# A second bias buffer and a norm in line in the last block, and scaled rows that stand behind VectorE's last instruction that is no tap

## The chip, the core and the metric

The kernel runs on one core of one Trainium2 chip. The time is device microseconds (us) of one execution; the median of several runs is compared. One core has five engines that matter here, each with a queue of its own and semaphores between them: TensorE (PE in the profile; PEld are its weight loads), VectorE (DVE), ScalarE (ACT), GpSimd (POOL) and SyncE (SP), which here only issues DMA transfers. Data are in DRAM, in the on-chip memory SBUF, and in PSUM, the banks that TensorE writes to.

## The reference, cut to what matters

One layer of a streaming encoder, for 2048 prompt frames and 64 sample frames, in float32 with D = 1024:

```python
h = rms_norm(x, norm1_g) * (1 + sc1) + sh1
glu_a, glu_b, q, k, v, g_conv, g_attn = split(h @ w_in)
u = glu_a * sigmoid(glu_b)                    # 512 channels
y = causal_depthwise_conv(u, width=31) + b_dw
y = silu(layer_norm(y, ln_g, ln_b))           # "the convolution's norm"
conv_out = y @ w_conv_out
q, k = rms_norm(q, per head), rms_norm(k, per head)   # 8 heads of 64
s = q @ k.T / 8 + rel_bias[clipped distance]; masked to 9 chunks of 64
attn_out = (softmax(s) @ v) @ w_attn_out
merged = sigmoid(g_conv) * conv_out + sigmoid(g_attn) * attn_out
x = x + gt1 * (merged @ w_o)
x = x + gt2 * swiglu_ffn(rms_norm(x) * (1 + sc2) + sh2)
```

The bias depends on the head and on the distance alone, so a tile of 128 queries against 640 keys needs one 128x640 tile of bias per head.

## The kernel before, in words

**Arithmetic.** Each float32 operand is split into a high and a low part (ScalarE copies the high part, rounded; VectorE or GpSimd subtracts it from the value), and a product is three products of parts. `split` and `low` do this; names end in `hi`/`lo`, `part_h`/`part_l`, `ph`/`pl`.

**Stages.** The first phase goes through the frames in four blocks b = 0 to 3 (`PBLOCKS`; the first holds the 64 sample frames and 512 prompt frames, the others 512). Each block has the stages q, 0, k, 1, v, 2, 3, g: the projections to q, k and v, between them the four channel tiles of the convolution's input (0 to 3), and at the end 16 gate tiles (g). The second phase (three blocks, `CBLOCKS`) reads the results back from DRAM: the norm's output from `c_d`, the attention's from `o_d`, the gates from `g_d`, and does merge, output projection and FFN. Phase one ends and phase two begins at about 1164 us of the span.

**What runs beside the projections.** Python generators, in lanes (`Lane`): the norm of the next block's rows, the scaling and storing of q, k, v rows (`work`), the attention's heads (`attn`, two at a time), the convolution (`conv`), and the convolution's norm (`tail`). After each TensorE instruction given, the planner (`Stream`) pumps the lanes: a generator goes on when the value it yielded is due. `stream.load[engine]` is the planner's own estimate of when the engine will be through with what it was given; `stream.when("act", "dve")` is the latest of several engines' estimates, and as a due time it is compared with TensorE's. `stream.at(t, f)` runs `f`, mostly a store, once TensorE's estimate has passed `t`.

**The order on the engines.** TensorE's instructions run in the order in which the program gives them (`manual_schedule` for PE). The order on VectorE, ScalarE, GpSimd and SyncE is chosen by the language's scheduler; `tc.issue_after(ins)` adds an edge: what is given under it stands behind `ins` in the order. `Meter` is the wrapper of each engine through which all compute instructions are given (its call is line 105, so nearly all rows of the profile say L105); it notes the instruction given last as `.last`.

**Scaled rows.** `qk_rows` handles a tile of 128 rows of q or k: ScalarE squares, VectorE sums per head (`ssq`, then `t`), GpSimd takes the root with a power (`r<-t,mhalf`), VectorE multiplies the rows by it (`kn<-kn,r`), TensorE transposes them (`store_kq`: `pt<-ident,kn`), ScalarE and VectorE split the result (`part_h`, `part_l`), SyncE stores it. The multiplication is given under `tc.issue_after(dve.last.ins)`: behind the instruction that VectorE was given last, whatever that is.

**The convolution.** `convolve` gives 31 instructions per channel tile on VectorE (`y<-u,wd,y`, a *tap* each; 0.8 us for 512 to 606 columns). They are the filling of VectorE: a tap is given whenever the planner has VectorE less than 2 us loaded, up to four in a row.

**The convolution's norm.** `conv_norm` waits until the block's taps are given, sums over the channels on GpSimd and TensorE (means, then squares), takes the root, and then goes through the four channel tiles one after the other: GpSimd multiplies (`y<-y,s`, all four given at the start), ScalarE's tanh (`ln<-y,lnh`), two steps of VectorE, the two parts (`part_h`, `part_l`), and stores to `c_d`. Between the steps it yields, so a tile takes four turns of the planner.

**Attention.** `attend` does one head: it waits until the head before has given all its scores; then `fetch` loads the bias (`load_bias`, two DMAs into the one tile `bias`, so they can't start before the last reader of the former bias is through) and q and k, and the scores wait for a due time `BIAS_LAG` = 6 us of the planner behind that load. For each of four tiles of 128 queries: scores (`sc`) on TensorE, sum with the bias and maximum in one VectorE instruction (`pr<-sc,bias`), exponential on ScalarE (`pr<-pr,sm`), transposes (`ptp`), parts, and the product with v (`po`). Two heads together give one 128x512 tile of output (`o_p`), split and stored to `o_d`. Blocks 0 to 3 have eight heads each, block 0 the sample's eight as well; a block's heads run beside the next block's stages, and block 3's beside its own gates.

**The last gate stage.** From the v stage of block 3 on, `attn` gives up to two steps per turn. In the gate stage `spare["open"]` is true for b >= 2 (the last block: until gate tile 6), which lets a head load the next head's q and k early. At gate tile 10 of block 3 the program gives all heads for which q and k were loaded early, closes the pool `wa` and takes its memory for the first loads of the merge. After the last gate the remaining head, taps and norm are drained, and the merge starts.

Of the kernel before, what the change touches and what calls it, by code (L numbers as in the profile page):

```python
# [8 lines left out]
F32 = mybir.dt.float32  # L9
# [613 lines left out]
def streaming_layer(ctx: ExitStack, tc: tile.TileContext, I, O):  # L623
# [392 lines left out]

    bias = wk.tile([P, 640], F32, name="bias")
    begun_rows = []
# [255 lines left out]
    def convolve(u, y, ct, b):  # L1274
# [13 lines left out]
        dve.tensor_scalar(y[:, ct, :n], u[:, :n], wd[:, ct, 0:1], bdw[:, ct : ct + 1], ALU.mult, ALU.add)  # L1288
        for k in range(1, TAPS):
            with tc.issue_after(ahead_of_taps[-1]) if ahead_of_taps else nullcontext():  # L1290
                dve.scalar_tensor_tensor(
                    y[:, ct, :n], u[:, k : k + n], wd[:, ct, k : k + 1], y[:, ct, :n], ALU.mult, ALU.add
                )
            yield

    def conv_norm(y, c0, n, t0):
        yv = y[:, :, c0 : c0 + n]
# [32 lines left out]
        yield stream.when("dve")  # L1330
        done = []
        for ct in range(4):
            gps.tensor_tensor(yv[:, ct], yv[:, ct], s[:, :n], ALU.mult)
            done.append(stream.when("pool"))
        for ct in range(4):
            yield done[ct]
            tmp = temp("ln")
            act.activation(tmp[:, :n], yv[:, ct], AF.Tanh, bias=lnh[:, 4 + ct : 5 + ct], scale=lnh[:, ct : ct + 1])
            yield stream.when("act")
            dve.tensor_scalar(yv[:, ct], yv[:, ct], lng[:, ct : ct + 1], lnb[:, ct : ct + 1], ALU.mult, ALU.add)  # L1340
            dve.scalar_tensor_tensor(tmp[:, :n], tmp[:, :n], 1.0, yv[:, ct], ALU.add, ALU.mult)
            yield stream.when("dve")
            hi, lo = parts()
            act.activation(hi[:, :n], tmp[:, :n], AF.Copy)
            yield stream.when("act")
            name = low(hi[:, :n], lo[:, :n], tmp[:, :n], n, TT_LESS)

            def store(ct=ct, hi=hi, lo=lo):
                for l, a in enumerate((hi, lo)):
                    nc.sync.dma_start(c_d[l, ct, :, t0 : t0 + n], a[:, :n].bitcast(F32))  # L1350

            stream.at(stream.when(name), store)

    def gates(b, free):
# [109 lines left out]
    def spans(b):  # L1464
# [4 lines left out]
        return SMP + QB * b, QB, CACHE + SMP + QB * b - past, QB + past  # L1469

    def load_bias(h):
        for r in (0, HD):
            nc.sync.dma_start(
                bias[r : r + HD, HD - r : 640 - r],
                bass.AP(tensor=rb_d.tensor, offset=rb_d.offset + 768 * h + HD, ap=[[1, HD], [1, 576]]),
            )
        return bias
# [33 lines left out]
    def attend(i):  # L1511
# [136 lines left out]
    for b, stage in ORDER:  # L1648
# [21 lines left out]
        elif stage == "g":  # L1670
            spare["open"] = b >= 2
            for g in gates(b, free):
# [20 lines left out]
        else:  # L1693
# [7 lines left out]
            if stage == 3:  # L1701
# [680 lines left out]
```

## Time and profile before

| | |
|---|---|
| median of 3 runs | 2945.38 us (2942.96 to 2947.97) |
| the profiled execution's own time | 2941.67 us |
| span of its profile | 2939.5 us |
| TensorE busy | 2889.3 us, 98% |
| VectorE busy | 2053.9 us, 70% |
| ScalarE busy | 1362.7 us, 46% |
| GpSimd busy | 1164.9 us, 40% |
| mean granted TensorE clock | 0.997 |

How to read it: the span runs from the first to the last instruction of the program in one profiled execution; the execution's own time is 2.2 us longer. The busy share is a mean over stages with different limits: TensorE has something to do nearly everywhere, so what matters is where it stands idle, and for what. A row of the waits names the instruction that came late to TensorE and the engine that it came from. A row of the timeline is: start in us, duration, engine, line, operation, output and inputs by the program's names, shape, and in square brackets the idle time just ahead and what ended it. The granted clock is the share of full speed that the chip granted TensorE in a stretch.

### The profile page before, as it was taken

What the parts mean: (1) busy time and instruction counts of PE and PEld (TensorE: products, weight loads), DVE (VectorE), ACT (ScalarE), POOL (GpSimd) and SP (SyncE); (2) the same over time, 40 slices, a digit from 0 to 9 for tenths busy, and PEclk for the clock granted to TensorE, in tenths of its full rate; (3) what the DMA queues carried; (4) which work ended last, traced back from release to release, by engine and by line L of the source; (5) the groups of instructions that cost most, each with busy time, mean ns of one, the idle gap of its engine ahead of it and who ended that gap; (6) DMA issues with size and microseconds to landing.
All of it is one profiled execution on the core that took longest, in us unless ns stands there. A gap on an engine that the chain in (4) does not pass through costs nothing.

```text
span 2939.5 us, 44832 instructions
## 1 busy us (share of the span) xinstructions
PE 2889.3 (98%) x16193; PEld 2587.5 (88%) x16193; DVE 2053.9 (70%) x3648; ACT 1362.7 (46%) x2453; POOL 1164.9 (40%) x753
## 2 busy tenths in 40 slices
PE   7999999999999999999999999999999999999999
PEld 5899777888888887988999998999999999999998
DVE  5897788668967885577777756666666557566666
ACT  3346543751564266563444345444444345444442
POOL 1201210111011002553566452366567742465667
PEclk9999999999999999999999999999999999999999
DMA  9989899978996987984444875332333965333333
GB/s 322 315 305 314 287 281 329 285 232 306 285 297 197 320 270 224 291 295 157 144 144 146 292 261 200 97 122 94 115 115 104 346 220 179 97 103 106 115 107 127
DMA packets 467067, 628.04 MB, mean 214 GB/s; under 512 B 36196, under 2 KB 314584, under 8 KB 466845
## 3 DMA queue, kind: packets, MB, share of 16 engines
q1 hardware_dynamic: 452944, 606.11, 63.4%
q10 hardware_dynamic: 13901, 19.08, 1.9%
q8 instruction: 127, 2.08, 0.3%
q14 instruction: 95, 0.78, 0.1%
HBM read 476.53 MB, written 148.54 MB: 213 GB/s over the span
## 4 chain that ended last, share of the span: by engine, by line
PE 47%; DVE 2%; ACT 1%; DMA 1%; issue 1%; POOL 0%; SPq 0%; ACTq 0%; DVEq 0%; POOLq 0%
PE ps L105 29%; PE pd L105 13%; PE pw L105 5%; DVE wlo L105 1%; ACT whi L105 1%; DVE ps L105 0%; DMA cin<-o_d 0%; DMA x<-x_d 0%; DVE acc L105 0%; ACT xn L105 0%; DMA wst<-in_w_ffn_in 0%; DMA wfo<-in_w_ffn_out 0%; DMA tg<-g_d 0%; DVE sums L105 0%; PE pt L105 0%
## 5 line engine op out<-in xcount | busy, mean ns | idle before, releaser
L105 PE MATMUL ps<-t,whi 128*128 128x384 f32 (+1 forms) x2112 | 502.0, 322 | 2.8 <-ACT u L105 1.7
L105 POOL TENSOR_TENSOR wlo<-wst,whi 128x1024 fp32r<-128x1024 f32 (+1 forms) x159 | 362.7, 2293 | 246.1 <-ACT whi L105 214.4
L105 ACT ACTIVATE whi<-wst 128x1024 fp32r<-128x1024 f32 (+1 forms) x265 | 258.3, 979 | 316.1 <-PE ps L105 129.6
L105 PE MATMUL ps<-b,whi 128*128 128x384 f32 (+1 forms) x1584 | 380.7, 325 | 6.4 <-DVE v L105 2.1
L105 PEld LDWEIGHTS ps<-t,whi 128*128 128x128 f32 x2112 | 367.8, 188 | 10.1 <-ACT u L105 3.9
L105 DVE SCALAR_TENSOR_TENSOR y<-u,wd,y 128x512 f32<-128x512 f32 (+1 forms) x480 | 370.1, 774 | 8.0
L105 PE MATMUL ps<-hh,whi 128*128 128x512 f32 (+2 forms) x992 | 362.8, 366 | 0.1
L105 DVE TENSOR_TENSOR acc<-acc,pd 128x512 f32<-128x512 f32 x482 | 322.2, 685 | 48.1 <-PE pd L105 45.6
L105 PE MATMUL ps<-hh,wlo 128*128 128x512 f32 (+2 forms) x992 | 345.2, 348 | 0.0
L105 PE MATMUL ps<-hl,whi 128*128 128x512 f32 (+2 forms) x992 | 344.5, 347 | 0.0
L105 PE MATMUL ps<-t,wlo 128*128 128x384 f32 (+1 forms) x1056 | 338.5, 321 | 0.0
L105 PE MATMUL pd<-whi,hid 128*128 128x512 f32 x912 | 297.9, 391 | 0.6 <-DVE hid L105 0.3
L105 PEld LDWEIGHTS ps<-b,whi 128*128 128x128 f32 x1584 | 276.9, 188 | 14.6 <-DVE v L105 3.2
L105 ACT ACTIVATE pr<-pr,sm 128x640 f32<-128x640 f32 (+3 forms) x272 | 201.9, 749 | 137.1 <-DVE sm L105 134.8
L105 PE MATMUL ps<-b,wlo 128*128 128x384 f32 (+1 forms) x792 | 256.1, 323 | 0.0
L105 POOL TENSOR_TENSOR r<-t,mhalf 128x1 f32<-128x1 f32 (+2 forms) x68 | 82.3, 1219 | 403.7 <-DVE t L105 377.8
L105 PEld LDWEIGHTS ps<-hh,wlo 128*128 128x128 f32 x992 | 186.5, 188 | 22.6
L105 DVE TENSOR_TENSOR wlo<-wst,whi 128x1024 fp32r<-128x1024 f32 (+1 forms) x106 | 135.9, 1286 | 100.3 <-ACT whi L105 98.9
L105 PEld LDWEIGHTS pd<-whi,hid 128*128 128x128 f32 x912 | 171.2, 188 | 37.2 <-DVE acc L105 1.8
L105 PEld LDWEIGHTS ps<-hh,whi 128*128 128x128 f32 x992 | 187.0, 189 | 18.2 <-issue 3.3
L105 PEld LDWEIGHTS ps<-hl,whi 128*128 128x128 f32 x992 | 187.4, 189 | 14.3 <-issue 1.7
L105 PEld LDWEIGHTS ps<-t,wlo 128*128 128x128 f32 x1056 | 198.2, 188 | 0.8
(233 smaller groups left out, 6309.6 us busy)
## 6 DMA issues: line engine op xcount, KB each, us to landing
whi<-w_din_h SPq DMA_DIRECT2D x72, 512.0 KB, 6.4
wlo<-w_din_l SPq DMA_DIRECT2D x72, 512.0 KB, 7.3
wst<-sum_d SPq DMA_DIRECT2D x131, 256.0 KB, 3.1
wfo<-in_w_ffn_out SPq DMA_DIRECT2D x64, 512.0 KB, 4.1
wmod<-in_w_ada SPq DMA_DIRECT2D x46, 512.0 KB, 8.8
sum_d<-ws SPq DMA_DIRECT2D x88, 256.0 KB, 2.0
wst<-in_w_ffn_in SPq DMA_DIRECT2D x85, 256.0 KB, 3.2
wst<-in_w_in SPq DMA_DIRECT2D x40, 512.0 KB, 6.0
```

Of the source, the lines that this page charges most:

```text
L105: self.last = f(*args, **kw)
```

## The change

Three parts.

*Scaled rows.* In `convolve` the tap no longer counts as the instruction given last: `dve.last` is put back to what it was before each tap. So `kn<-kn,r` in `qk_rows`, and the other places that use `dve.last`, stand behind the last instruction of VectorE that is not a tap (nor the first product of a channel tile's convolution, which still counts).

*A second bias buffer.* In the last block's gate stage, up to gate tile 6, `spare["open"]` has the value "wide". As a head starts its scores there, it loads not only the next head's q and k but also its bias, into a second tile taken from pool `wa` under tag "x" (three slots that also hold v rows and some k rows). The two corners of it that the loads don't reach are filled with a large negative number, once. A head that finds its bias loaded takes the due time of that load.

*The norm's line.* In the last block, `conv_norm` no longer goes through the channel tiles one after the other. In round i = 0 to 6 it gives the parts and stores of tile i-3, the two VectorE steps of tile i-2, the tanh of tile i-1 and GpSimd's product of tile i, and yields once between rounds, until the planner's latest estimate of ScalarE, VectorE and GpSimd. In the other blocks the same steps are given in the same order as before.

```diff
@@ convolve
         for k in range(1, TAPS):
+            other = dve.last
             with tc.issue_after(ahead_of_taps[-1]) if ahead_of_taps else nullcontext():
                 dve.scalar_tensor_tensor(
                     y[:, ct, :n], u[:, k : k + n], wd[:, ct, k : k + 1], y[:, ct, :n], ALU.mult, ALU.add
                 )
+            dve.last = other
             yield
@@ conv_norm
-    def conv_norm(y, c0, n, t0):
+    def conv_norm(y, c0, n, t0, line=False):
...
+        tmps = [None] * 4
+
+        def over(ct):
+            gps.tensor_tensor(yv[:, ct], yv[:, ct], s[:, :n], ALU.mult)
+
+        def swish(ct):
+            tmps[ct] = temp("ln")
+            act.activation(tmps[ct][:, :n], yv[:, ct], AF.Tanh, bias=lnh[:, 4 + ct : 5 + ct], scale=lnh[:, ct : ct + 1])
+
+        def times(ct):
+            tmp = tmps[ct]
+            dve.tensor_scalar(yv[:, ct], yv[:, ct], lng[:, ct : ct + 1], lnb[:, ct : ct + 1], ALU.mult, ALU.add)
+            dve.scalar_tensor_tensor(tmp[:, :n], tmp[:, :n], 1.0, yv[:, ct], ALU.add, ALU.mult)
+
+        def give(ct):
+            tmp = tmps[ct]
+            hi, lo = parts()
+            act.activation(hi[:, :n], tmp[:, :n], AF.Copy)
+            if not line:
+                yield stream.when("act")
+            name = low(hi[:, :n], lo[:, :n], tmp[:, :n], n, TT_LESS)
...
+            stream.at(stream.when(name), store)
+
+        if line:
+            for i in range(7):
+                if 0 <= i - 3:
+                    yield from give(i - 3)
+                for step, ct in ((times, i - 2), (swish, i - 1), (over, i)):
+                    if 0 <= ct < 4:
+                        step(ct)
+                if i < 6:
+                    yield stream.when("act", "dve", "pool")
+            return
@@ load_bias
+    second = {}
+
     def load_bias(h):
+        bias = first_bias
+        if spare["open"] == "wide" and now["bias"] is not None and now["bias"][1] is first_bias:
+            bias = second.get("tile")
+            if bias is None:
+                bias = second["tile"] = wa.tile([P, 2, 512], F32, tag="x", name="bias", bufs=3)[:].rearrange("p a b -> p (a b)")[:, :640]
+                for r, c in ((0, 0), (HD, 576)):
+                    dve.memset(bias[r : r + HD, c : c + HD], BIG)
@@ fetch
-            if now["bias"] is None or now["bias"][0] != h:
+            told = now.pop("next", None)
+            landed = stream.load["pe"] + BIAS_LAG
+            if told is not None and told[0] == i:
+                now["bias"], landed = told[1:3], told[3]
+            elif now["bias"] is None or now["bias"][0] != h:
                 now["bias"] = h, load_bias(h)
...
-            loaded[i] = max(stream.load["pe"] + BIAS_LAG, ahead_qk.get(i, stream.load["pe"] + lag))
+            loaded[i] = max(landed, ahead_qk.get(i, stream.load["pe"] + lag))
@@ attend
             fetch_qk(i + 1)
             ahead_qk[i + 1] = stream.load["pe"] + QK_LAG
+            if spare["open"] == "wide":
+                now["next"] = i + 1, order[i + 1][1], load_bias(order[i + 1][1]), stream.load["pe"] + BIAS_LAG
@@ the stages
-            spare["open"] = b >= 2
+            spare["open"] = b >= 2 and ("wide" if b == len(PBLOCKS) - 1 else "narrow")
...
-                    tail.add(conv_norm(y, 0, QB, lo))
+                    tail.add(conv_norm(y, 0, QB, lo, b == len(PBLOCKS) - 1))
```

More of the change, by code (lines that the diff above doesn't have):

```diff
@@ L1015, in first_block @@
         next(taps, None)
-    bias = wk.tile([P, 640], F32, name="bias")
+    first_bias = bias = wk.tile([P, 640], F32, name="bias")
     begun_rows = []
@@ L1336, in conv_norm @@
             yield done[ct]
-            tmp = temp("ln")
-            act.activation(tmp[:, :n], yv[:, ct], AF.Tanh, bias=lnh[:, 4 + ct : 5 + ct], scale=lnh[:, ct : ct + 1])
+            swish(ct)
             yield stream.when("act")
-            dve.tensor_scalar(yv[:, ct], yv[:, ct], lng[:, ct : ct + 1], lnb[:, ct : ct + 1], ALU.mult, ALU.add)
-            dve.scalar_tensor_tensor(tmp[:, :n], tmp[:, :n], 1.0, yv[:, ct], ALU.add, ALU.mult)
+            times(ct)
             yield stream.when("dve")
[L1343 to L1352, printed above, removed]
+            yield from give(ct)
     def gates(b, free):
```

5 lines of the change are left out of this document (4 added, 1 removed).

## The prediction

> **What bounds the kernel now.** I read the page first, then the waits of TensorE, then the timelines of the two places where it waits longest and the change acts.
>
> ```profile
> span 2939.5 us, 44832 instructions
> PE 2889.3 (98%) x16193; PEld 2587.5 (88%) x16193; DVE 2053.9 (70%) x3648; ACT 1362.7 (46%) x2453; POOL 1164.9 (40%) x753
> ...
> PE pt L105 <- DVE kn L105: 6.1, 2, 4.0
> PE ps L105 <- DVE t L105: 5.8, 5, 3.4
> PE sc L105 <- DVE sm L105: 2.7, 5, 1.3
> ```
>
> TensorE is busy for 98% of the span: 50 us are idle in all (2939.5 - 2889.3), and its work is the same after the change. So the change can only win or lose idle time of TensorE, and the clock that goes with it. The wait rows (engine and tile, who ended the wait, us in total, times, longest) name rows kn (6.1 us in two waits) and t (longest 3.4 us).
>
> ```profile
> 1157.02 0.33 PE L105 MATMUL ptp<-ident,pr 128*128 128x128 f32 x1 [0.50 <-ACT pr L105]
> 1158.76 0.50 PE L105 MATMUL po<-pl,vv 128*128 128x512 f32 x1 [0.22 <-DVE pl L105]
> 1162.55 0.45 PE L105 MATMUL po<-pl,vv 128*128 128x384 f32 x1 [0.28 <-DVE pl L105]
> 1164.57 0.41 PE L105 MATMUL ps<-cin,whi 128*128 128x320 f32 x1 [1.40 <-DVE o_p L105]
> 1175.29 0.90 PE L105 MATMUL ps<-cin,whi 128*128 128x320 f32 x2 [3.42 <-DVE t L105]
> ```
>
> These are the five waits at the passage from the projections to the merge (start, duration, instruction, idle time before it and its releaser). The first three and the fourth are the last attention head, alone on TensorE when the gates are through (0.50 + 0.22 + 0.28 = 1.00 us, and 1.40 us for its output o_p, whose PSUM bank the merge takes over). The fifth is VectorE's first merge product. Why that was late:
>
> ```profile
> 1169.59 2.79 DVE L105 TENSOR_TENSOR part_l<-ln,part_h 128x512 fp32r<-128x512 f32 x1 [0.70 <-DMA o_d<-part_l]
> 1174.75 0.49 DVE L105 SCALAR_TENSOR_TENSOR t<-tg,ps 128x320 f32<-128x320 f32 x1 [2.38 <-DMA c_d<-part_l]
> ...
> 1172.40 0.32 SPq L1350 DMA_DIRECT2D c_d<-part_l  x1
> ...
> L105 ACT ACTIVATE ln<-y,lnh x4: 800/808/821, 1130.1 to 1163.8; 128x512 f32<-128x512 f32 x4
> ```
>
> The convolution's norm is still at its last channel tile. Its four tanhs run from 1130.1 to 1163.8, one per 11.2 us, though each is 0.81 us of work; the last lower part ends at 1172.38, its store is issued at 1172.40, and t, which takes over that memory, starts when the store has landed.
>
> ```profile
> 1170.53:1173.95 3.42, 1.34 (x10) 1.08 (x8) 1.84 (x1) 0.00 (x0) 1.29 (x1) 1.00 0.23 84
> 1173.95:1180.78 6.83, 5.49 (x20) 5.49 (x21) 3.43 (x8) 0.86 (x3) 0.00 (x0) 0.50 0.91 273
> 1180.78:1187.61 6.83, 6.83 (x48) 6.80 (x48) 2.50 (x8) 3.53 (x5) 5.79 (x3) 1.00 1.03 341
> ```
>
> Stretches of time: length, busy time and instructions of TensorE, weight loads, VectorE, ScalarE, GpSimd, then the granted clock. After 3.42 us with only 1.34 busy the clock is 0.50 for 6.83 us. There 20 matmuls took 5.49 us; the next 6.83 us hold 48 of the same, so 20 are worth 2.85 us, and the half clock cost 2.64 us.
>
> **The change part by part: the norm's line.** The steps and their instructions are the same 4 x (GpSimd multiply, tanh, two VectorE steps, two halves, two stores); only the order is new: one round does the next step of up to four tiles, and there are 6 pauses in place of 15. A pause is now as long as the planner holds the fullest of three engines loaded, for which I take 3 us, from the longest chain of a round (the 0.81 tanh and, as an estimate from t's 0.49 on 320 columns, 0.5 to 0.8 for each of its three VectorE instructions). From the multiplies at 1126.9 (below) that gives the last tile at about 1126.9 + 6 x 3 = 1145, its stores landed some 6 us later, 1151: ahead of the last gate. So t and the queue no longer wait: -3.42 us and, with the idle stretch gone, -2.64 us.
>
> ```profile
> 1126.89 4.66 POOL L105 TENSOR_TENSOR y<-y,s 128x512 f32<-128x512 f32 x4
> 1169.43 2.39 POOL L105 TENSOR_TENSOR wlo<-wst,whi 128x1024 fp32r<-128x1024 f32 x1 [5.71 <-ACT whi L105]
> c_d<-part_h SPq DMA_DIRECT2D x16, 256.0 KB, 6.1
> ```
>
> The four multiplies took 4.66 us in a row and now run beside VectorE's products. The long part_l above (2.79 us) ends 0.56 us after GpSimd's wlo of 1169.43 does (1171.82). The Trainium skill, "SBUF — State Buffer", section "Who interferes with whom", says that a VectorE instruction with two SBUF inputs and a GpSimd instruction that reads SBUF lock each other out for a whole instruction; this row agrees, and by that rule the line meets up to three such locks of about 1.2 us, 3.6 us on a chain that by the sum ends 11 us early, so the sum stays.
>
> **The second bias buffer.** A head's bias is loaded one head ahead, into a spare 128x1024 slot, in the gate stage's first part; two memsets of 64x64 on VectorE are added at the first of them (under the 0.49 us of t above each, with VectorE a quarter idle there), the number of loads stays.
>
> ```profile
> 1075.52 0.81 DVE L105 CUSTOM_DVE_ANT_0 pr<-sc,bias 128x640 f32<-128x640 f32 x1
> 1076.36 1.10 SPq L1473 DMA_DIRECT2D bias<-rb_d  x2
> 1081.58 0.81 DVE L105 CUSTOM_DVE_ANT_0 pr<-sc,bias 128x640 f32<-128x640 f32 x1
> 1122.84 0.83 DVE L105 CUSTOM_DVE_ANT_0 pr<-sc,bias 128x640 f32<-128x640 f32 x1 [0.18 <-DMA bias<-rb_d]
> ```
>
> A head's last score maximum is at 1075.52, the next bias is asked for at 1076.36, the next head starts at 1081.58, 6.06 us on. From there to 1122.84 two heads pass, 20.6 us each; less a turn of 6.06 that is 14.6 us for three steps from tile to tile, 4.9 us at most. So 1 to 2 us are won per head, and more where a head waits for the bias itself (that of 1122.84), whose planned time now counts from a load one head earlier: an estimate of 15 us over the last five, between 6 and 25. The last head, whose o_p let the merge go on at 1164.57, is through near 1150, beside the gates: -1.00 us, and of the 1.40 I keep half (the merge's first bank may then wait for ScalarE to read the last gate; bounds 0 and 1.40): -0.70 us. The loads are moved past the q, k and v loads on SyncE's queue; 1.10 us of issue per head either way, with nobody waiting there.
>
> What it adds: heads that stand closer. ScalarE's work per head is 11.1 us:
>
> ```profile
> L105 ACT ACTIVATE pr<-pr,sm 128x640 f32<-128x640 f32 x56 | 46.0, 827 | 20.3 <-DVE sm L105 19.9
> L105 ACT ACTIVATE ph<-ptp 128x512 fp32r<-128x512 f32 x38 | 22.0, 593 | 13.6 <-PE ptp L105 13.5
> L105 ACT ACTIVATION_READ_ACCUMULATOR pr<-pr,sm 128x1 f32 x28 | 5.2, 187 | 0.0
> L105 ACT ACTIVATE other<-po 64x512 f32<-64x512 f32 x7 | 4.2, 593 | 0.2
> ```
>
> (46.0 + 22.0 + 5.2 + 4.2)/7 heads. With 18 us from head to head that leaves room; with 13 and a gate's 0.6 it is 90% full. The trace does not show such a stretch. Bounds: 0, and the longest wait for a maximum (1.3 us) once in five heads, 6.5 us. I take 1.0, nearer the short end, since TensorE's row of waits has only 2.7 us of that kind for all 40 heads.
>
> **Scaled rows.** In block 0 to 3 rows of the k stage are queued behind the last tap given. The one that matters:
>
> ```profile
> 99.88 0.17 DVE L105 TENSOR_SCALAR t<-ssq 128x8 f32<-128x8 f32 x1
> 100.20 3.76 POOL L105 TENSOR_TENSOR r<-t,mhalf 128x8 f32<-128x8 f32 x2 [4.30 <-DVE t L105]
> 105.83 0.69 DVE L105 TENSOR_TENSOR part_l<-pt,part_h 128x512 fp32r<-128x512 f32 x1 [1.59 <-ACT part_h L105]
> 107.80 0.84 DVE L105 SCALAR_TENSOR_TENSOR y<-u,wd,y 128x606 f32<-128x606 f32 x1
> 108.56 0.69 DVE L105 TENSOR_TENSOR kn<-kn,r 128x512 f32<-128x512 f32 x1
> 109.40 0.41 PE L105 MATMUL pt<-ident,kn 128*128 128x128 f32 x2 [2.15 <-DVE kn L105]
> 106.44:209.05 102.61, 100.46 (x658) 92.62 (x657) 100.67 (x151) 38.13 (x66) 12.58 (x10) 1.00 0.91 312
> 212.82 0.44 PE L105 MATMUL sc<-kk,q 128*128 128x384 f32 x1 [0.26 <-DVE sm L105]
> ```
>
> This root was done at half of 3.76 us, 102.1, the row was scaled at 108.56 behind a tap, and TensorE stood 2.15 us. Freed of the tap it fits into the 1.59 us in which VectorE waited, and the 2.15 us go. But from 106.44 to 209.05 VectorE is busy for 100.67 of 102.61 us, and at 212.82 TensorE waits for it: what it won it gives back there, save the 0.69 us that moved into the idle slot. Against that, a row that is placed ahead of its root holds every tap behind it:
>
> ```profile
> 918.84 0.69 DVE L105 TENSOR_TENSOR kn<-kn,r 128x512 f32<-128x512 f32 x1 [1.81 <-POOL r L105]
> ```
>
> 1.81 us once, and block 0 has three such rows: +5.4 us less the 1.59 us idle and the 0.69, about +3. Bounds -2.15 and +3, middle near 0; I take 0. In blocks 1 to 3 no wait of TensorE hangs on such a row (the second kn wait, 3.96 us at 360.51, stands behind a store, below, not behind a tap).
>
> **Sum.** -3.42 - 2.64 - 1.00 - 0.70 + 1.0 + 0 = -6.8 us. The profiled execution took 2941.67 us (2.2 us around its span), 3.7 us less than the median of 2945.38. Against the median: 2938.6 us, -0.23%. What a measurement tells from no change is about 0.2%, 5.9 us, so faster begins at 2939.5 and slower at 2951.3.
>
> **The rivals.** First: the passage waits for something else. Weights (wlo, 2.39 us above) or the gate rows tg of the merge, loaded only two tiles ahead, may be late next. Then the 3.42 us and the clock are won in part; at half of the 6.06 us the time is 2941.6. For it: ScalarE's and VectorE's work there is unchanged; against it: SyncE's queue is freed too, as its store at 1172.40 no longer holds it.
>
> Second: the root holds VectorE in block 0, the +3 us above: 2941.6.
>
> Third, on the slower side: halves that wait for stores. The norm's halves share two buffers with the heads' outputs and the queries; the line gives them 3 us apart, so a buffer is asked for again after 6 us, and a store lands after 6.1 us at the median.
>
> ```profile
> 358.26 0.69 ACT L105 ACTIVATE part_h<-pt,gqk 128x512 fp32r<-128x512 f32 x1 [1.10 <-DMA c_d<-part_h]
> 362.54 0.69 ACT L105 ACTIVATE part_h<-pt,gqk 128x512 fp32r<-128x512 f32 x1 [3.59 <-DMA c_d<-part_h]
> 360.51 0.63 PE L105 MATMUL pt<-ident,kn 128*128 128x128 f32 x4 [3.96 <-DVE kn L105]
> ```
>
> This is block 0's norm drained in a burst: ScalarE stood 1.10 and 3.59 us for stores, VectorE behind it, TensorE 3.96 us. With 2.64 us of half clock that is 6.6 us each time; two such stops in the last block cost 13.2 us, and with the gain of 6.8 the time is 2951.8. It decides when a head is still under way as the halves come; by the sum the heads end near 1150 and the halves come from 1136, so it can be, though gates alone would not mind.
>
> That the change does little (the order on the engines falls out as before): 2944.
>
> The Trainium skill, "TensorE: Matmul & The Clock Gate", section "What's actually happening", has the clock fall after an idle window of 3.4 us that runs freely. Here it fell 2.08 us into the idle time, after a window that was 39% busy; by the page's rule a stop of 3.96 us need not cost a half clock at all, and the slower rival would come to 7.9 us, 2946.5.
>
> **How the numbers follow.** Forecast 0.42 (2934 to 2940); passage in part 0.20; root in block 0 0.10; little changed 0.08; halves that wait for stores 0.20 (two stops; three would be 2958). Faster by over 0.2%: the forecast, 0.40 (its upper end lies past the bound); within 0.2%: 0.40, that end and the three cases in between; slower 0.20. For 8 in 10 the range goes from 2932 (nothing paid for closer heads, and the 2.15 us kept in part) to 2952 (two stops). The forecast's own range is 2934 to 2940.
>
> **What would show it.** Right: no wait of TensorE above 1 us between 1150 and 1185 and a clock of 1.00 there; the last tanh of the norm before 1150; the last o_p before the last gate; the wait at 107 gone and a wait for a maximum near 183 to 213 grown. Wrong: VectorE idle for r in the k stages; part_h waiting for c_d; new waits for pr, sm or pl in the last block; TensorE waiting for m, tg or weights after 1165. An order of instructions on VectorE that changes elsewhere, in blocks 1 and 2, would be outside all of this and could cost a few us either way.

## The result

Over 20 runs each, the changed kernel takes 2948.35 us (median; 2942.93 to 2954.69) and the kernel before 2943.03 us (2939.88 to 2947.97). The ratio is 1.0017, with an interval of 1.0011 to 1.0023: about 5.0 us slower, by less than the 0.2% that the prediction took as its bound. Forecast were 2938.6 us, 6.8 us faster than before, with a range from 2932 to 2952. The time lies in the range, but on the other side of the kernel before.

The profiled execution of the changed kernel took 2944.85 us (before: 2941.67). From its page, the span and the engines, and from the waits of TensorE the three rows that answer to those shown of before:

```profile
span 2943.0 us, 44833 instructions
PE 2887.1 (98%) x16193; PEld 2585.9 (88%) x16193; DVE 2054.9 (70%) x3650; ACT 1362.3 (46%) x2453; POOL 1163.7 (40%) x753
PE pt L105 <- DVE kn L105: 8.1, 2, 6.6
PE ps L105 <- DVE t L105: 4.0, 4, 3.2
PE sc L105 <- DVE sm L105: 4.0, 4, 2.1
```

The work is the same and TensorE is idle for 55.9 us (2943.0 - 2887.1), 5.7 us more than before. The waits for rows (kn) grew from 6.1 to 8.1 us, those for maxima (sm) from 2.7 to 4.0, and the one for t that the change was expected to remove went only from 3.4 to 3.2. The waits themselves, from TensorE's timeline (start, duration, instruction, in brackets the idle time ahead of it and who ended it):

```profile
126.29 0.30 PE L105 MATMUL pt<-ident,kn 128*128 128x128 f32 x1 [1.49 <-DVE kn L105]
308.85 0.80 PE L105 MATMUL sc<-kk,q 128*128 128x256 f32 x2 [2.13 <-DVE sm L105]
367.00 0.45 PE L105 MATMUL pt<-ident,kn 128*128 128x128 f32 x1 [6.57 <-DVE kn L105]
1165.96 0.39 PE L105 MATMUL ps<-cin,whi 128*128 128x320 f32 x1 [1.08 <-DVE row L105]
1176.49 0.90 PE L105 MATMUL ps<-cin,whi 128*128 128x320 f32 x2 [3.24 <-DVE t L105]
```

Set side by side by TensorE's instructions, the changed kernel is 1.1 us behind at 50 us (waits at the kernel's start, which differ from execution to execution), 1.3 us ahead at 108 us (the wait of 2.15 us is gone), 0.35 behind at 126, 2.35 at 309, 6.5 at 367, 3.5 at 401, 4.2 at 975, 1.4 at 1166 and 2.4 at TensorE's last instruction (3.5 by the span). So the loss is made between 126 and 370 us, in block 0. The last block, for which two of the three parts were made, wins 2.8 us, of which the second phase gives 1.0 back.

At the passage to the merge, groups of ScalarE's and VectorE's instructions in the changed kernel (count, least/median/longest duration in ns, first and last start):

```profile
L105 ACT ACTIVATE ln<-y,lnh x4: 802/807/816, 1152.2 to 1162.8; 128x512 f32<-128x512 f32 x4
L105 DVE SCALAR_TENSOR_TENSOR y<-u,wd,y x63: 730/752/755, 999.7 to 1109.9; 128x512 f32<-128x512 f32 x63
L105 DVE CUSTOM_DVE_ANT_0 pr<-sc,bias x28: 760/818/827, 1033.9 to 1144.1; 128x640 f32<-128x640 f32 x28
```

the same two groups of VectorE before the change:

```profile
L105 DVE SCALAR_TENSOR_TENSOR y<-u,wd,y x60: 730/752/929, 1002.7 to 1089.2; 128x512 f32<-128x512 f32 x60
L105 DVE CUSTOM_DVE_ANT_0 pr<-sc,bias x28: 808/815/828, 1029.1 to 1153.4; 128x640 f32<-128x640 f32 x28
```

and the timeline of GpSimd and VectorE after it:

```profile
1166.43 8.00 POOL L105 TENSOR_TENSOR wlo<-wst,whi 128x1024 fp32r<-128x1024 f32 x3 [11.07 <-ACT whi L105]
1166.90 5.30 DVE L105 TENSOR_TENSOR part_l<-ln,part_h 128x512 fp32r<-128x512 f32 x2 [0.49 <-ACT part_h L105]
1175.94 0.49 DVE L105 SCALAR_TENSOR_TENSOR t<-tg,ps 128x320 f32<-128x320 f32 x1 [3.34 <-DMA c_d<-part_h]
```

The heads do end earlier: their last maximum is at 1144.1 in place of 1153.4. The four tanhs do run in a line, 10.6 us from first to last in place of 33.7. But the last tap of the convolution moved from 1089.2 to 1109.9, the norm behind it starts that much later, and its last two lower parts take 5.30 us for the two, beside three subtractions of GpSimd. The store of these parts is as late as before, t waits for it, and the clock (third column from the right, ahead of DMA share and GB/s) falls as before:

```profile
1171.97:1175.38 3.41, 1.28 (x9) 1.01 (x7) 0.64 (x2) 0.00 (x0) 2.46 (x1) 1.00 1.01 381
1175.38:1182.21 6.83, 5.72 (x21) 5.72 (x22) 3.61 (x10) 1.09 (x3) 0.00 (x0) 0.50 0.95 286
```

### The profile page after: what moved, and what is told of

It is laid out like the page before. It is cut to its first block, busy times and chain, and to the rows that moved or that the text cites. A ratio compares the mean times of both kernels' runs of the same rounds, so it can differ in the third digit from the quotient of the medians.

```text
span 2943.0 us, 44833 instructions
## 1 busy us (share of the span) xinstructions
PE 2887.1 (98%) x16193; PEld 2585.9 (88%) x16193; DVE 2054.9 (70%) x3650; ACT 1362.3 (46%) x2453; POOL 1163.7 (40%) x753
## 4 chain that ended last, share of the span: by engine, by line
PE 47%; DVE 2%; ACT 1%; DMA 1%; issue 1%; POOL 0%; SPq 0%; ACTq 0%; DVEq 0%; POOLq 0%
PE ps L105 28%; PE pd L105 13%; PE pw L105 5%; DVE wlo L105 1%; ACT whi L105 1%; DVE ps L105 0%; DMA cin<-o_d 0%; DMA x<-x_d 0%; DMA wst<-in_w_conv_out 0%; ACT xn L105 0%; DMA tg<-g_d 0%; DMA wfo<-in_w_ffn_out 0%; DVE acc L105 0%; DVE sums L105 0%; PE pt L105 0%
```

## The experiments

Times are medians, each beside runs of the kernel before on the same chip (2942.4 to 2943.3 us). Brackets hold the 95% interval of the ratio, and a difference with a sign is that ratio in us. "The page" below is that of the profile.

### The parts one by one

**Rows alone.** The change with its first part only.

```diff
+            other = dve.last
             ... the tap ...
+            dve.last = other
```

> The scaled rows alone. Theory 1 (the new order on VectorE in blocks 0 and 1 is where the time goes): slower than before by 3.5 to 5 us, as the changed kernel's profile is 3.5 us behind at 470 us of the span; the wait for kn near 360 us stands at 5 us or more. Theory 2 (the closer heads of the last block are the cost): within 1.5 us of before. My forecast for this part was 0, between -2.15 and +3.

Measured: 2949.71 us, ratio 1.0023 [1.0015, 1.0032]: +6.8 us. The first part, which the sum took at nothing, costs no less than the whole change.

**Bias buffer alone.** The second tile and the early load, neither rows nor line.

```diff
-            spare["open"] = b >= 2
+            spare["open"] = b >= 2 and ("wide" if b == len(PBLOCKS) - 1 else "narrow")
```

> The second bias buffer alone. Theory 1: within 1.5 us of before: what the last head no longer waits (2.4 us) is lost again as the taps, and so the norm, come later. Theory 2: slower by 3 us or more, with the norm's first tanh some 20 us later than at 1130 and a longer wait for t. My forecast for this part was -0.7 (-1.00 -0.70 +1.0).

Measured: 2945.2 us, 1.0008 [0.9999, 1.0017]. The interval leaves both theories open. The convolution's last tap starts at 1103.2 in place of 1089.2, the norm's first tanh at 1147.9 in place of 1130.1, and TensorE waits 3.44 us for t, as before.

**Line alone.**

```diff
-                    tail.add(conv_norm(y, 0, QB, lo))
+                    tail.add(conv_norm(y, 0, QB, lo, b == len(PBLOCKS) - 1))
```

> The norm's line alone. If the line does what I forecast: the last tanh ends before 1150, the waits for t (3.4 us) and the half clock behind it (2.64 us) go, 4 to 6 us faster. If its place depends on when the taps are through and not on its own pauses: the last tanh stays near 1160, t waits as before, within 1.5 us of before.

Measured: 2943.03 us, 1.0001 [0.9993, 1.0010]. The tanhs are through before 1150, as the prediction asked, though the last tile's lower part starts at 1152.45 and not at about 1145; and yet nothing is won. ScalarE's group:

```profile
L105 ACT ACTIVATE ln<-y,lnh x4: 802/802/836, 1132.8 to 1144.5; 128x512 f32<-128x512 f32 x4
```

the longest of TensorE's waits there:

```profile
1162.07 0.47 PE L105 MATMUL ptp<-ident,pr 128*128 128x128 f32 x1 [2.44 <-ACT pr L105]
```

and two stretches of time (columns as in those shown of before):

```profile
1158.20:1161.60 3.40, 1.18 (x7) 0.89 (x7) 1.44 (x7) 3.38 (x7) 2.35 (x1) 1.00 0.22 89
1161.60:1168.40 6.80, 6.09 (x24) 5.20 (x25) 2.77 (x4) 3.52 (x6) 0.00 (x0) 0.50 0.32 105
```

The wait of 3.42 us for t is gone, as forecast. In its place the last head is later, TensorE runs out of other work around 1160 while ScalarE is busy for 3.38 of 3.40 us, and the half clock falls there, 12 us earlier than before, with another 3.4 us of it at 1171.9.

**Bias buffer and line, no rows.** The change without the two lines of the first experiment.

> Bias buffer and line together, without the scaled rows. Theory 1: -1 to +1.5 us against before, that is the changed kernel less the 3.5 to 5 us of the rows; the norm's first tanh near 1150, part_l locked for 5 us and t waiting 3 us as in the changed kernel. Theory 2: as slow as the changed kernel, +4 to +6 us.

Measured: 2942.32 us, 1.0000 [0.9992, 1.0009], where the prediction had -6.8 us for these two. So the loss of the whole change comes with the rows.

### Where the rows cost

**Rows in block 0 only, and rows in the later blocks only.**

```diff
-            dve.last = other
+            if not b:
+                dve.last = other
```

(the second: `if b:`)

> The scaled rows' edge dropped in block 0 alone (three rows move; blocks 1 to 3 as before). If the price comes from block 0's rows and what the scheduler then orders otherwise behind them: as slow as with the rows of all blocks, 1.0015 to 1.003 of before (+4.5 to +9 us), the waits for sm near 307 us and for kn near 361 us at 2.5 and 6.5 us again. If it comes from the nine rows of blocks 1 to 3: within 1.5 us of before.

> The scaled rows' edge dropped in blocks 1 to 3 alone. Counterpart of the run before: within 1.5 us of before if block 0's three rows carry the price; +4.5 us or more if not. Up to 390 us of the span the waits are those of before (kn 4.0 near 357, none of 2 us for sm).

Measured: block 0 only 2950.97 us, 1.0025 [1.0014, 1.0036]; later blocks only 2942.61 us, 0.9999 [0.9991, 1.0008]. All of it comes from block 0, where only the rows of the k stage are freed of taps. From VectorE's and TensorE's timeline of the rows alone:

```profile
126.15 0.41 PE L105 MATMUL pt<-ident,kn 128*128 128x128 f32 x2 [1.88 <-DVE kn L105]
309.59 0.29 DVE L105 CUSTOM_DVE_ANT_0 pr<-sc,bias 128x128 f32<-128x128 f32 x1 [0.33 <-DMA bias<-rb_d]
309.94 0.39 PE L105 MATMUL sc<-kk,q 128*128 128x256 f32 x1 [2.63 <-DVE sm L105]
366.69 0.75 DVE L105 SCALAR_TENSOR_TENSOR part_l<-pt,gqk,part_h 128x512 fp32r<-128x512 f32 x1 [3.76 <-DMA c_d<-part_l]
```

In the k stage itself much is as the prediction had it: VectorE stands for the root three times (1.53 us at 96, 0.25 at 102, 0.47 at 129) and once for a store (1.67 at 112), the 2.15 us at 107 are gone, and TensorE gives them back, 1.88 us at 126. At that point the kernel is 0.2 us behind, and it had been 0.5 us behind from its start on, so the stage has won 0.3. The loss is further on: +0.8 us at 282, +3.5 at 310, +7.7 at 368, then +5.1 at 402 (a wait of 1.25 us is gone there), +6.8 at 424 (a wait of 1.59 us for a weight's load), +7.6 at 979. All traces agree on the stretch: from 96 to 402 us the seven kernels that keep the waits of before in block 0 stay within 0.8 us of the kernel before, and the ten others lose 1.3 to 8.7. Two waits make most of it, for a maximum at 307 (2.63 us, and a half clock of 3.4 us) and for a row at 361 (6.57 us, as in the whole change), 200 us after the last instruction that was moved. What they hang on is in the issues of SyncE's queue (start, duration, line, transfer). With the rows alone:

```profile
164.18 2.57 SPq L1459 DMA_DIRECT2D kk<-k_d  x2
171.39 0.38 SPq L1465 DMA_DIRECT2D vv<-v_d  x1
173.67 0.58 SPq L384 DMA_DIRECT2D wst<-in_w_in  x1
305.68 1.09 SPq L1511 DMA_DIRECT2D bias<-rb_d  x2
361.20 0.32 SPq L1357 DMA_DIRECT2D c_d<-part_h  x1
361.61 0.38 SPq L479 DMA_DIRECT2D whi<-w_dqkv_h  x1
362.09 0.39 SPq L1357 DMA_DIRECT2D c_d<-part_l  x1
```

and before:

```profile
103.42 0.60 SPq L1429 DMA_DIRECT2D kk<-q_d  x1
108.92 1.63 SPq L1430 DMA_DIRECT2D kk<-k_d  x2
165.41 1.18 SPq L384 DMA_DIRECT2D wst<-in_w_in  x1
171.15 0.37 SPq L1436 DMA_DIRECT2D vv<-v_d  x1
300.76 1.09 SPq L1473 DMA_DIRECT2D bias<-rb_d  x2
356.89 0.32 SPq L1350 DMA_DIRECT2D c_d<-part_l  x1
```

with VectorE's row for the next use of that buffer:

```profile
359.02 0.75 DVE L105 SCALAR_TENSOR_TENSOR part_l<-pt,gqk,part_h 128x512 fp32r<-128x512 f32 x1 [1.13 <-ACT part_h L105]
```

Before, the q and k loads of the first sample head are issued from 103 to 110 us; with the rows moved they stand at 164 to 173. The load of the raw weights (wst) was ahead of the v load, which waits until 171 in both kernels, and is now behind it: 173.67 in place of 165.41. SyncE's queue stays some 3 to 5 us late up to 312, the bias at 300.76 among it (305.68), and the maximum at 309.59 waits for that bias. At 361 the load of a weight's high part (512 KB, by the page's sizes) now stands between the two stores of the norm's third tile: the lower store is issued at 362.09 and VectorE, which takes its buffer over, starts at 366.69 (the last row of VectorE above), 4.6 us later; before, store and next use were 2.1 us apart (356.89 to 359.02), with only the store of the higher part just ahead and VectorE waiting for ScalarE, not for the store.

### Which of it is the cause

**The maximum and the store.** The rows alone, with VectorE's four subtractions of the norm (`y<-y,pm`) tied behind the head's maximum, so that it isn't late at 307; and a second kernel in which also the weight load at 361 is tied behind the lower store.

```diff
+            with tc.issue_after(ahead_of_taps[-1]):
-            dve.tensor_tensor(yv[:, ct], yv[:, ct], pm[:, :n], ALU.subtract)
+                dve.tensor_tensor(yv[:, ct], yv[:, ct], pm[:, :n], ALU.subtract)
@@ the second kernel, norm's store and the load of stored weights
+                if (ct, t0) == (2, SMP):
+                    W.stand = tc.issue_after(sent.ins)
...
+            with self.__dict__.pop("stand", None) or nullcontext():
```

> The scaled rows alone, with one edge added: the four y<-y,pm of the convolution's norm stand behind the last score maximum given, as they stood before. If the wait of 2.6 us for sm near 307 us is the flipped order of these five instructions: that wait falls below 0.7 us and the kernel gains 2 to 4.5 us on the rows alone (about 1.0008 to 1.0016 of before); the wait for kn near 361 us stays at 6.5. If the wait there comes from VectorE's load as such: unchanged, 1.0023.

> As the run before, and one more edge on SyncE: the load whi<-w_dqkv_3_h no longer stands between the two stores c_d<-part_h and c_d<-part_l of the norm's third tile in block 0, but behind both. If the 512 KB load ahead of the low part's store is what makes the wait for kn 6.6 us instead of 4.0: it falls to 4.5 us or less and another 2 to 3 us come back (1.0000 to 1.0008 of before). If the store is late for another reason: 6.5 us still, and the time as in the run before.

Measured: 2948.25 us, 1.0017 [1.0009, 1.0026], and 2950.0 us, 1.0023 [1.0013, 1.0033]. Neither separated the theories, because neither edit removed its wait. In the first, TensorE's wait at 307 stayed, 2.76 us; VectorE now stood for the bias itself:

```profile
310.24 0.29 DVE L105 CUSTOM_DVE_ANT_0 pr<-sc,bias 128x128 f32<-128x128 f32 x1 [2.00 <-DMA bias<-rb_d]
```

So the four subtractions ahead of the maximum were filling a wait, and the late bias load is what counts there. In the second, the 512 KB load went behind the store, and a load of v rows (256 KB) took its place:

```profile
362.07 0.39 SPq L1469 DMA_DIRECT2D vv<-v_d  x1
362.55 0.51 SPq L1359 DMA_DIRECT2D c_d<-part_l  x1
365.94 0.75 DVE L105 SCALAR_TENSOR_TENSOR part_l<-pt,gqk,part_h 128x512 fp32r<-128x512 f32 x1 [2.56 <-DMA c_d<-part_l]
```

It was 3.4 us from issue to the next use of the buffer, between the 2.1 us without a load ahead and the 4.6 us behind 512 KB. TensorE's wait there was 5.40 us in place of 6.55 in the kernel with the first edit alone; in the time this does not show.

**The head's loads.** Two kernels from both sides. One is the rows alone, with the first sample head's four q and k loads on ScalarE's queue, so that nothing on SyncE stands behind these four; the other is the kernel before, with no row moved, and the same four loads made late.

```diff
+        queue = nc.scalar if (x, h) == ("s", 0) else nc.sync
-            nc.sync.dma_start(q2[...], q_d[...])
-            nc.sync.dma_start(kk[...], k_d[...])
+            queue.dma_start(q2[...], q_d[...])
+            queue.dma_start(kk[...], k_d[...])
@@ the other, from before
+        with tc.issue_after(now["sent"]) if (x, h) == ("s", 0) else nullcontext():
...
+                now["sent"] = nc.sync.dma_start(kk[...], k_d[...]).ins
```

> The scaled rows alone, and the four loads of q and k of the first sample head go on ScalarE's queue instead of SyncE's. In the run with the rows alone the scheduler issues these four at 166 to 173 us on SyncE, ahead of a weight load; in the kernel before they were issued at 103 to 110 us. Theory 3 (SyncE's queue runs some 5 us late from 173 us on because of them, and the bias load and the stores behind it are what TensorE waits for at 307 and 361 us): the lag is gone, the waits for sm near 307 and kn near 361 us are at 0.7 and 4.0 to 4.5 us, the time is back within 2 us of before. Theory 1b (VectorE's own load and order is the cause): 1.0015 to 1.003 of before as with the rows alone.

> The kernel before, with one edge: these four loads stand behind the last load of the first prompt head on SyncE, as they come to stand in the changed kernel; no row on VectorE is moved by hand. Theory 3: SyncE runs late from 173 us on, the waits near 307 and 361 us appear, 3 to 7 us slower than before (1.001 to 1.0025). Theory 1b: within 1.5 us of before.

Measured: the other queue 2946.87 us, 1.0013 [1.0004, 1.0023], +3.8 us in place of +6.8; late loads alone 2949.93 us, 1.0021 [1.0012, 1.0031], +6.2 us. From TensorE's timeline, and a stretch of time, of the kernel with late loads:

```profile
367.12 0.45 PE L105 MATMUL pt<-ident,kn 128*128 128x128 f32 x1 [6.57 <-DVE kn L105]
```

```profile
362.40:376.10 13.70, 8.98 (x30) 7.82 (x31) 6.36 (x13) 3.68 (x7) 0.00 (x0) 0.50 1.02 368
```

and of the other queue, TensorE's two long waits and VectorE's row behind the first:

```profile
316.26 1.95 DVE L105 TENSOR_TENSOR part_l<-o_s,part_h 128x64 fp32r<-128x64 f32 x1 [1.11 <-ACT part_h L105]
320.05 0.41 PE L105 MATMUL pt<-ident,x_t 128*128 128x128 f32 x2 [2.45 <-DVE x_t L105]
368.96 0.66 PE L105 MATMUL pt<-ident,kn 128*128 128x128 f32 x2 [6.51 <-DVE kn L105]
```

Late loads are enough to bring the whole loss with no row moved: the wait for a row at 361 grows to the same 6.57 us. In that trace VectorE's, ScalarE's and GpSimd's instructions stand in the order of before up to 301 us, and SyncE's alone differ, from 103 us on. The forecast wait at 307 did not come, though; one of 2.45 us at 318 did.

Late loads are not the only way to the loss. With the loads off SyncE's queue the wait at 307 goes, the one of 2.45 us at 318 comes here too, and the 6.5 us at 361 stay; by its own forecast (back within 2 us of before) theory 3 fails here. About half comes back at the median, though the intervals of the two (1.0004 to 1.0023 and 1.0015 to 1.0032) overlap. What is left is visible in the trace. At 318 the 128x64 lower part above takes 1.95 us in place of 0.21 before, beside a GpSimd subtraction of 2.38 us that ends 0.08 us ahead of it, and the scaling of x_t behind it 1.77 us in place of 0.74, beside a GpSimd sum. At 361 the 512 KB load stands between the two stores here as well (stores issued at 362.06 and 362.95, the load at 362.47). It does so in all eight traces with a wait of 6.5 us or more there, and in none of the eight with 3.9 to 4.0 us. (With the one row of column 256, below, it is issued 1.5 us ahead of the lower store, and the wait is 4.24 us.)

**The same queue for the whole change.**

> The changed kernel, with the four loads of the first sample head on ScalarE's queue. Theory 3: 4 to 6 us faster than the changed kernel, within 2 us of before. Theory 1b: 1.0012 to 1.0022 of before, as the changed kernel.

Measured: 2946.5 us, 1.0012 [1.0003, 1.0021]. Of +5.0 us some 1.5 are taken back, no more than the intervals allow for chance; the 4 to 6 us of theory 3 did not come.

**One row at a time.** The kernel before, with only the row of k column 256, 320 or 704 in block 0 placed behind the last instruction that is no tap; the diff shows the first.

```diff
+        free = dst is k_d and col == 256 and dve.last is taps_seen["tap"]
-        with tc.issue_after(dve.last.ins):
+        with tc.issue_after((taps_seen["other"] if free else dve.last).ins):
```

> The kernel before with one scaled row freed of the tap ahead of it: the sample's k row of block 0 (column 256; in the run with all rows VectorE stood 1.53 us for its root at 96.6). If any of the three rows is enough to turn the scheduler's order over: SyncE's loads of the first sample head come late and the kernel is 3 to 7 us slower (1.001 to 1.0025). If only the row that TensorE waited for matters: within 2 us of before.

> The same with the k row of column 320 alone, the one for which TensorE stood 2.15 us at 107. By my forecast's mechanism: that wait goes and about 1.5 us of it come back as waits for VectorE before 213, within 2 us of before. If the order that the scheduler makes of the rest is what counts: 3 to 7 us slower, with waits near 307 to 318 and 6.5 us near 361.

> The same with the k row of column 704 alone (scaled at 128.6 before). TensorE did not wait for it: by the forecast's mechanism within 1 us of before; if the order of the rest is what counts, it can cost as much as the others, and the lag of SyncE's queue from 173 us on tells whether it does.

Measured: 2946.79 us, 1.0013 [1.0004, 1.0022]; 2945.53 us, 1.0005 [0.9996, 1.0014]; 2943.42 us, 0.9998 [0.9989, 1.0007]. A wait of TensorE from the first:

```profile
113.65 0.66 PE L105 MATMUL pt<-ident,kn 128*128 128x128 f32 x2 [5.41 <-DVE kn L105]
```

Three rows, three outcomes. Column 256 makes a new wait of 5.41 us on the spot; column 320 removes the 2.15 us at 107 as the prediction had it and still has a long wait near 361, 6.65 us, with a time that can't be told from no change; column 704 leaves the waits as they were (2.15 us at 110 among them). With column 704 SyncE's instructions stand in the order of before through the whole kernel and only VectorE's differ; with the other two SyncE's differ from 99 and 106 us on. The cost isn't that of a row held for its root (at most 1.53 us here), but of what each new order puts elsewhere.

### What the passage still hung on

**Lower parts of five merge weights on VectorE,** in the kernel with bias buffer and line but without the rows, and the same edit in the kernel before.

```diff
-        on_dve = key[0] == "in" or key[0] == "qkv" and (passing or key[1]) or turn % 2
+        on_dve = key[0] == "in" or key[0] == "ca" and i < self.keys.index(("ca", 0)) + 5 or key[0] == "qkv" and (passing or key[1]) or turn % 2
```

> Bias buffer and line together (no scaled rows), and the low parts of the first five weights of the merge are made by VectorE instead of GpSimd. If the two last part_l of the norm are late because GpSimd's subtractions lock them out (5.30 us for two in the changed kernel, 0.69 each elsewhere): they take 0.69 us each, the wait for t (3.1 us) falls below 1 us, and the kernel is 2 to 5 us faster than bias and line without this edit (0.9983 to 0.9995 of before). If it is the stores' way alone: the wait stays above 2 us.

> The kernel before, with the low parts of the first five weights of the merge made by VectorE, as in the fastest run so far (0.9985 with bias buffer and line). If the lock at the passage is all that the line could win: 3 to 5 us faster by itself (0.9983 to 0.9990). If the edit needs the line, because in the kernel before the norm's last tile comes late by its own pauses: within 2 us of before, with t still waiting 2 us or more.

Measured: 2938.34 us, 0.9985 [0.9976, 0.9994], 5.0 us faster than the kernel before by the medians and 4.4 by the ratio; in the kernel before, 2948.95 us, 1.0010 [1.0001, 1.0019]. The first beats both kernels. Its lower parts as a group:

```profile
L105 DVE TENSOR_TENSOR part_l<-ln,part_h x4: 682/686/693, 1155.3 to 1166.1; 128x512 fp32r<-128x512 f32 x4
```

the rows of VectorE and TensorE in which what is late now stands:

```profile
1182.15 0.50 DVE L105 SCALAR_TENSOR_TENSOR ps<-tg,ps 128x320 f32<-128x320 f32 x1 [4.91 <-DMA tg<-g_d]
1183.53 0.56 PE L105 MATMUL ps<-cin,whi 128*128 128x320 f32 x2 [1.34 <-DVE t L105]
```

and the stretch of the passage:

```profile
1170.00:1190.00 20.00, 18.66 (x125) 18.13 (x124) 8.89 (x21) 7.69 (x10) 9.51 (x4) 1.00 0.97 322
```

With no GpSimd subtraction beside them, all four lower parts take 0.69 us, the store is in time, the wait of 3.1 us for t and the half clock behind it are gone, and what is left is 1.34 us for the gate rows tg (the forecast was below 1) and 1.45 us at 1191 for a weight's lower part. So the two subtractions of 5.30 us, beside GpSimd's three of 8.00, kept the gain of the other two parts from showing. In the kernel before the edit costs 2.9 us (0.3 to 5.6 by the interval), and t still waits 1.99 us. So it needs the order that bias buffer and line give together; which of the two it needs was not run.

## Why the prediction was wrong

Two steps failed: the scaled rows, taken at 0, cost 6.8 us, and the 6.8 us that bias buffer and line were to win came out at 0. That the time still lies inside the range is luck: the range reached up to 2952 for halves that wait for stores in the last block, which did not come. Its lower end does not follow from the terms given for it either: 2938.6 less 1.0 and 2.15 is 2935.5, not 2932.

**Scaled rows: "I take 0", bounds -2.15 and +3.** This step turned the sign: measured +6.8 us alone, outside the bounds. Its local working held. The 2.15 us were won, VectorE stood for roots for 2.25 us, and TensorE gave most of the time back, though at 126 and not at 212 as named: at 126 it was 0.2 to 0.35 us behind the kernel before, after 0.5 to 1.1 us before the stage. What it left out is that the order of the other instructions follows from this one: it counted who waits for the moved row, not which loads SyncE's queue would then issue later. The four loads that moved 60 us, the raw weights behind a v load that waits, and the 512 KB load ahead of a store were none of its terms. The late loads without any row moved bring +6.2 us, so that a changed order on SyncE's queue is enough is shown; that these four loads are needed for it is refuted by the other queue, where a lower part held up beside GpSimd at 318 and the 512 KB load between the stores at 361 are left. How the loss divides between these places is read from single traces and not shown, and what makes the scheduler choose each order is open.

The second rival had the right place, block 0, with the root itself as the cause and +3 us as its price; the runs give the place, but the roots held VectorE for 2.25 us only, and at 126 nothing was lost by them. The last sentence on what would make the prediction wrong named a changed order elsewhere that could cost a few us, for blocks 1 and 2 and for VectorE; it came in block 0 and on SyncE.

**Bias buffer: -1.70, +1.0 for closer heads.** The direction held: the last maximum came 9.3 us earlier, inside the bounds of 6 to 25 but short of the 15. The waits of 0.50, 0.22 and 0.28 us went; at the merge's first instruction 1.08 us, now for `row`, stand in place of the 1.40 of which the sum kept half. Not named was what the heads push aside: the convolution's taps share VectorE with them, and the last tap came 20.7 us later (14.0 with the buffer alone). The norm waits for the taps, and its multiplies, at 1126.9 in the prediction's working, started at 1146.0. The term was mis-sized by its effect on the next one. Alone it measured +2.4 us, within an interval of -0.3 to +5.0.

**The line: -3.42 and -2.64.** Alone, the line came early enough: multiplies at 1129.6, the last lower part at 1152.45 (forecast 1126.9 and 1145), and the wait for t went. The gain didn't come, since a wait of 2.44 us on the last head, with the same half clock, took its place. With the bias buffer the line starts some 20 us later and its last halves meet GpSimd's subtractions. Here a sentence of the prediction failed by itself: the lock of VectorE and GpSimd was priced, at 3.6 us, "on a chain that by the sum ends 11 us early, so the sum stays". The two subtractions lost 3.9 us to it (5.30 - 2 x 0.69). That this is close to the price is chance, since the price was for GpSimd's multiplies of the norm and the partner was its subtractions for the weights; and the chain wasn't early. The Trainium skill, "SBUF — State Buffer", section "Who interferes with whom", has such instructions exclude one another for a whole instruction; the 5.30 us agree, and so do the 0.69 us each once the other engine's subtractions are gone.

**The first rival** (the passage waits for weights or gate rows next, half of the gain) is what stands behind the lock: 1.34 us for tg once it is removed, and 1.05 us for a weight's lower part in the changed kernel (1.45 once the lock is removed). **The third** (halves waiting for stores, twice 6.6 us in the last block) did not come as described: ScalarE's halves there wait for a store once, 0.36 us; t does, as before. **That little changes** fits bias buffer and line together, 1.0000, though not for its reason: the order did change, but TensorE's waits from 1150 to 1210 us add up to 5.5 us in place of 5.8.

**The half clock.** The prediction cited a rule by which a stop of 3.96 us need not cost a half clock. No trace here has such a stop near 360 us without one; the next section has the numbers. Since it priced a rival alone, the sum is not touched.

## What to carry to other kernels

Where a scheduler or a shared DMA queue orders the work, the price of moving one instruction is not only its own wait: list which loads and stores would change places behind it, up to a few hundred us later, and give that a bound of its own: here it came to 6.8 us, against a local bound of 3. Before a step is costed at nothing because its chain ends early, ask what the other parts of the change do to the time at which that chain starts. And a store that frees a buffer is worth keeping ahead of a large load on the same queue: at most 2.1 us to the buffer's next use with no load just ahead, 3.4 behind 256 KB, 4.6 behind 512 KB.

## What the runs showed of the hardware

The same wait does not always cost the same clock. The wait for a row near 360 us is 3.98 us in the kernel with bias buffer and line, and 4.01 us in the kernel with the line alone; up to there the two issue the same instructions in the same order. The first, its wait and the stretch behind it:

```profile
362.78 0.66 PE L105 MATMUL pt<-ident,kn 128*128 128x128 f32 x2 [3.98 <-DVE kn L105]
```

```profile
362.60:366.00 3.40, 3.22 (x11) 2.77 (x12) 0.69 (x2) 0.69 (x1) 0.00 (x0) 0.51 1.06 368
```

and the second:

```profile
361.73 0.66 PE L105 MATMUL pt<-ident,kn 128*128 128x128 f32 x2 [4.01 <-DVE kn L105]
```

```profile
359.50:369.70 10.20, 7.97 (x27) 7.02 (x28) 5.79 (x12) 3.23 (x7) 0.00 (x0) 0.50 1.04 340
```

Half clock (0.51 and 0.50) for 3.4 us in one and for 10.2 us in the other; in the kernel before it was 6.8 us. After a wait of some 6.5 us it was 6.8 us in four of the traces (the whole change, the rows alone, and both with the other queue), 10.2 us in three (rows in block 0 only, the maximum tied first, column 320) and 13.7 us with the late loads, always a multiple of 3.4. Near 308 us a half clock of 3.4 us also followed shorter waits, 1.21 us with bias buffer and line and 0.74 us with the rows in the later blocks only. In each trace the half clocks also begin whole steps of 3.41 us apart (with the line alone at 359.5, 1161.6 and 1171.9: 235 and 3 steps). The Trainium skill, "TensorE: Matmul & The Clock Gate", section "What's actually happening", has a window of about 3.4 us that runs freely; the multiples agree, and how a wait falls into the windows may decide how many are lost. At half speed 3.4 us more cost up to 1.7 us, so one kernel's runs could differ by several us at a handful of such waits; the spread was 8.1 us for the kernel before and 11.8 us for the changed one. That the phase of this window is what makes that spread is argued here and not shown.
